# A three-column tile of norm weights padded to 32 columns in a one-core hybrid attention layer

## The chip, the core and the metric

The kernel runs on one core of one Trainium2 chip. Its time is the device time of one execution in microseconds (us); where several runs are given, their median counts.

## The reference

The reference is one layer of a generator over 1024 latent tokens with 256 context tokens in front, 1024 channels wide. The tokens are normalised and modulated, and one wide projection makes the inputs of two branches. One branch is a gated linear attention (GLA) of 4 heads, run in chunks in both directions. The other is a differential attention of 8 heads. Both are normalised, gated, projected, merged and projected once more.

```python
pl = project(modulate(x, sh_x, sc_x), w_in[layer])
pc = project(modulate(ctx, sh_c, sc_c), w_in[layer])
...
o_gla = bidir_gla(q, k, v, la_f, la_b, s_f, s_b)
o_diff = diff_attention(q1, q2, jnp.concatenate([ck1, k1], axis=2), jnp.concatenate([ck2, k2], axis=2),
                        jnp.concatenate([cv, dv], axis=2), lam)
...
a = merge_heads(rms_norm(o_gla) * gla_gain) * jax.nn.silu(gla_gate)
b = merge_heads(rms_norm(o_diff) * diff_gain * (1 - lam_init)) * jax.nn.silu(diff_gate)
y = jax.nn.sigmoid(m_gla) * (a @ w_br_gla) + jax.nn.sigmoid(m_diff) * (b @ w_br_diff)
x = x + g_x * (y @ w_out)
```

The tile that the change touches holds `gla_gain` (256 values, two columns of 128) and `diff_gain` (128 values, one column).

## The kernel before, in words

Every product of two matrices is made in float32r from operands that are split into a high and a low part: `mm3` issues three matmuls, high by high, high by low and low by high. Each matmul has a stationary operand of 128 columns, loaded into the array ahead of it (PEld in the profile), and a moving operand of mostly 512 columns, in some places 256. In the profile's names the moving operand comes first: `mm<-w,g` has the moving operand `w` and the stationary operand `g`. Numbers are left out of tile names, so `g` is a buffer of the tag `g5`, `l` of `l5`, `h` of `h0` or `h1`, `s` of `s5`, `b` of `b1`, `at` of `at4` or `at2`.

The work goes through four stages, which overlap at their edges:

- Projections (to about 500 us). `pairs` and `jobs` multiply the normalised tokens (`h0`, `h1`, `hk`) by split weights (`w`). Four of the output groups are made by a seven-product scheme on halves of the matrices, and there the stationary operands are sums of token blocks in `g5`.
- GLA and the remaining projections (about 500 to 905 us). GLA's tiles are `gv`, `gkt`, `gqe` and others; between its steps the projections `mm<-w,h` and `mm<-h,w` run.
- Differential attention (about 905 to 1450 us). Scores are `s<-hk,aq`, transposes `b<-ident,e`, products with the values `b<-at,vv`. In between run the branch projections of GLA's output, `mb<-h,wt`.
- Output (about 1450 us to the end): `mc`, `mz` and `mb` with operands `h`, `wt`, `xa`, `aq`, `ya`, `yb`, `yc`.

A driver in the kernel simulates the engines with fixed costs while the program is built, and the order of instructions on each engine comes from it. It does not look at addresses.

On-chip memory is given out by pools, which is what matters here. The pool of constants (`self.c`, pool `cst`) lies at the low end of each partition, and the pools marked `left` in `POOLS` are stacked behind it, upward: `sb` (`raw`, `h0`, `h1`), `sbK` (`hk`), `sbA` (`w`, `p`, `pl`), later `sbB` (`vv`, `at4`, `at2`, `ac`, `b1k`) and `sbC` (`ya`, `yb`, `o`). The pools marked `right` are stacked downward from the top of memory: `sbE` with one unused tile of 96 bytes, then `sbA1` (`g5`, `l5`, `x2`, `x4`), `sbA2` (GLA's tiles), `sbG` (`aq`, `xa`), `sbW` (`wt`, `ft`), `sbF` (`e5`), `sbD` (`yc`, `yd`, `wr`). Tiles start at multiples of 32 bytes.

The tile of the change, `gcol`, is filled in `consts_late` by two small DMAs, scaled there by GpSimd, and read later as a column of scales: by `pl<-tp,gcol` after GLA and by `b1k<-b,gcol` after attention.

Of the kernel before, what the change touches and what calls it, by code (L numbers as in the profile page):

```python
# [20 lines left out]
P = 128  # L21
# [211 lines left out]
class Hybrid:  # L233
# [222 lines left out]
    def consts_late(self):  # L456

        nc, a = self.nc, self.a

        def bc(ap, n):  # L460
            return ap.unsqueeze(0).to_broadcast([P, n])

        self.gains = g = self.c("gains", [P, 2, 2, 64])
        for i, nm in enumerate(("diff_q_norm", "diff_k_norm")):
            self.dma(g[:, i, 0], bc(a[nm][0], 64))
        self.gcol = self.c("gcol", [P, 3])
        self.dma(self.gcol[:, 0:2], a["gla_norm"][0].rearrange("(x p) -> p x", p=P))
        self.dma(self.gcol[:, 2:3], a["diff_norm"][0].rearrange("(x p) -> p x", p=P))
        yield from self.acq("p", 2)
        lp = self.t("p", [P, 4, 64])  # L470
        self.dma(lp, a["diff_lambda"][0].unsqueeze(0).to_broadcast([P, 4, 64]))
        yield self.d.when(lp)

        self.pool.tensor_scalar(g[:, 0, 0], g[:, 0, 0], 0.125, 0.0, ALU.mult, ALU.add)
        for i in range(2):
            gi, gr = (g[:, i, x].rearrange("p (x h e) -> p x h e", h=2, e=16) for x in range(2))
            for hh in range(2):
                self.pool.tensor_scalar(gr[:, :, hh], gi[:, :, 1 - hh], 1.0, 0.0, ALU.mult, ALU.add)
        self.pool.tensor_scalar(self.gcol[:, 0:2], self.gcol[:, 0:2], 0.5, 0.0, ALU.mult, ALU.add)
        self.pool.tensor_scalar(self.gcol[:, 2:3], self.gcol[:, 2:3], 1.0 - LAM_INIT, 0.5, ALU.mult, ALU.mult)  # L480
        lm = self.t("p", [P, 2, 64])
        self.dve.tensor_tensor(lm, lp[:, 0::2], lp[:, 1::2], ALU.mult)
        ls = self.c("ls", [P, 2])
        self.rel("p", self.dve.tensor_reduce(ls, lm, AX.X, ALU.add), 2)
        yield self.d.when(ls)
        yield self.act.activation(ls, ls, AF.Exp)
        self.nlam = self.c("nlam", [P, 1])
        self.dve.tensor_tensor(self.nlam, ls[:, 1:2], ls[:, 0:1], ALU.subtract)
        self.dve.tensor_scalar(self.nlam, self.nlam, LAM_INIT, None, ALU.subtract)
# [2321 lines left out]
```

## Time and profile before

| what | value |
|---|---|
| median of 3 runs | 1627.58 us (1626.64 to 1632.06) |
| the profiled execution's own time | 1629.48 us |
| its span in the profile | 1627.8 us |
| TensorE matmul (PE) busy | 1599.2 us, 98% |
| TensorE weight load (PEld) busy | 1328.7 us, 82% |
| VectorE (DVE) busy | 1248.3 us, 77% |
| ScalarE (ACT) busy | 858.4 us, 53% |
| GpSimd (POOL) busy | 581.7 us, 36% |
| 16 DMA engines, share of the span | 65.8% |
| granted TensorE clock | 0.997 of full |

The profile is of one execution. A row of the timeline gives the start of a batch of like instructions, its length up to the end of the last one, and their number. Since a matmul's end is modelled and it overlaps the next one, the rate of a batch is read from the start of the batch to the start of the batch behind it, divided by the number.

### The profile page before, as it was taken

To read this page: it belongs to the slowest core of one execution; us is meant where nothing else is said; L and a number is where in the kernel's file an instruction comes from. 1 tells how busy PE (TensorE), PEld (TensorE's weight loads), DVE (VectorE), ACT (ScalarE), POOL (GpSimd) and SP (SyncE) were. 2 spreads that over 40 slices of the span, in tenths; PEclk is the share of its full clock that TensorE was granted. 3 is DMA by queue.
4 is the path that set the end of the run, shared out by engine and by line. 5 is a ranking of instruction groups with operands and counts; after the bars stand their busy time and mean duration, and the time that the engine had idled before them with its cause. 6 is when DMAs were issued, how large, how long until landed. Compare 5 with 4: busy or idle time off the path is not lost.

```text
span 1627.8 us, 24787 instructions
## 1 busy us (share of the span) xinstructions
PE 1599.2 (98%) x8333; PEld 1328.7 (82%) x8333; DVE 1248.3 (77%) x2209; ACT 858.4 (53%) x1771; POOL 581.7 (36%) x631
## 2 busy tenths in 40 slices
PE   7999999999999999999999999999999999999999
PEld 3788888888888888888878788888888888887887
DVE  4687957674756889879887588787878888878994
ACT  4676644433443453565645466565665565656331
POOL 1500001000001657445554146566755666660000
PEclk9999999999999999999999999999999999999999
DMA  8576898988978577776648644454577554357662
GB/s 304 193 244 232 324 321 303 323 323 293 315 263 272 157 216 240 220 236 204 207 140 221 192 117 135 124 160 129 151 241 239 157 144 131 107 177 249 217 205 94
DMA packets 275182, 346.72 MB, mean 213 GB/s; under 512 B 24136, under 2 KB 174320, under 8 KB 275056
## 3 DMA queue, kind: packets, MB, share of 16 engines
q1 hardware_dynamic: 275056, 345.14, 65.8%
q8 instruction: 66, 1.08, 0.3%
q14 instruction: 60, 0.49, 0.1%
HBM read 235.49 MB, written 109.58 MB: 212 GB/s over the span
## 4 chain that ended last, share of the span: by engine, by line
PE 85%; DVE 5%; ACT 3%; POOL 2%; issue 2%; DMA 2%; SPq 0%; ACTq 0%; POOLq 0%; DVEq 0%
PE mm L349 30%; PE mb L349 9%; PE tp L349 7%; PE s L349 7%; PE mc L349 7%; PE b L349 6%; PE gs L349 4%; PE go L349 4%; PE b L375 4%; PE gt L349 3%; DVE sm L201 2%; PE mz L349 2%; PE tp L375 2%; ACT e L201 1%; POOL at L201 1%
## 5 line engine op out<-in xcount | busy, mean ns | idle before, releaser
L349 PE MATMUL mm<-w,h 128*128 128x512 f32 x912 | 227.6, 398 | 0.0
L349 PE MATMUL mb<-h,wt 128*128 128x512 f32 x840 | 224.2, 402 | 0.8 <-DVE ft L201 0.5
L201 ACT ACTIVATE e<-s,sm 128x1280 f32<-128x1280 f32 x128 | 169.5, 1329 | 73.7 <-DVE sm L201 70.6
L201 DVE TENSOR_REDUCE sm<-s 128x1 f32<-128x1024 f32 (+1 forms) x192 | 193.5, 1036 | 17.9 <-PE s L349 14.1
L349 PEld LDWEIGHTS mm<-w,h 128*128 128x128 f32 x912 | 167.4, 189 | 32.2
L201 POOL TENSOR_TENSOR at<-ac,at 128x512 fp32r<-128x512 f32 x128 | 188.8, 1475 | 10.7
L349 PEld LDWEIGHTS mb<-h,wt 128*128 128x128 f32 x840 | 151.2, 188 | 31.8 <-ACT ft L201 1.0
L349 PE MATMUL s<-hk,aq 128*128 128x512 f32 x744 | 170.5, 365 | 0.7 <-ACT e L201 0.4
L201 POOL TENSOR_SCALAR at<-ac 128x512 fp32r<-128x512 f32 x128 | 96.8, 756 | 194.7 <-ACT ac L201 194.5
L349 PE MATMUL mm<-h,w 128*128 128x512 f32 x672 | 165.4, 398 | 0.3 <-DVE h L201 0.3
L349 PEld LDWEIGHTS mm<-h,w 128*128 128x128 f32 x672 | 125.2, 191 | 26.5 <-DVE h L201 1.0
L349 PEld LDWEIGHTS s<-hk,aq 128*128 128x128 f32 x744 | 117.2, 188 | 18.7 <-ACT e L201 3.9
L201 DVE TENSOR_TENSOR w<-raw,w 128x512 fp32r<-128x512 f32 x128 | 89.3, 720 | 54.6 <-ACT w L201 54.2
L349 PE MATMUL b<-at,vv 128*128 128x256 f32 x960 | 130.1, 287 | 1.1 <-ACT ac L201 0.8
L201 POOL TENSOR_TENSOR sm<-sm,nhalf 128x2 f32<-128x2 f32 (+2 forms) x94 | 108.0, 1149 | 44.7 <-DVE sm L201 39.5
L349 PEld LDWEIGHTS b<-at,vv 128*128 128x128 f32 x960 | 119.8, 191 | 3.0 <-ACT ac L201 1.0
L201 DVE SCALAR_TENSOR_TENSOR e<-e,sm,e 128x1280 f32<-128x1280 f32 x64 | 120.3, 1879 | 0.7
L201 ACT ACTIVATE ac<-b 128x512 f32<-128x512 f32 x122 | 72.1, 597 | 81.9 <-PE b L375 81.5
L201 ACT ACTIVATE w<-raw 128x512 fp32r<-128x512 f32 x128 | 76.8, 625 | 65.7 <-DMA raw<-in_w_in 18.7
L349 PE MATMUL mm<-w,g 128*128 128x512 f32 x432 | 108.9, 396 | 0.0
L349 PEld LDWEIGHTS mm<-w,g 128*128 128x128 f32 x432 | 81.0, 187 | 20.2 <-issue 0.5
L201 ACT ACTIVATE p<-mm 128x512 f32<-128x512 f32 (+1 forms) x104 | 60.2, 586 | 69.1 <-PE mm L349 54.3
(352 smaller groups left out, 3102.8 us busy)
## 6 DMA issues: line engine op xcount, KB each, us to landing
raw<-in_w_in SPq DMA_DIRECT2D x62, 512.0 KB, 5.2
g<-d_s SPq DMA_DIRECT2D x32, 640.0 KB, 6.8
gv<-d_v SPq DMA_DIRECT2D x80, 256.0 KB, 3.9
g<-d_s SPq DMA_DIRECT2D x32, 512.0 KB, 6.2
aq<-d_qT SPq DMA_DIRECT2D x124, 128.0 KB, 3.4
d_dv<-pl SPq DMA_DIRECT2D x40, 256.0 KB, 4.1
d_v<-pl SPq DMA_DIRECT2D x40, 256.0 KB, 2.6
d_kT<-pl SPq DMA_DIRECT2D x40, 256.0 KB, 2.7
```

The source lines that it names most:

```text
L201: self.ins = f(out, *args, **kw).ins
L349: self.ins = self.nc.tensor.matmul(out, lhsT, rhs, start=start, stop=stop, skip_group_check=more).ins
L375: self.nc.tensor.transpose(out, src, self.ident[:n, :n])
```

## The change

The tile `gcol` is made 32 columns wide instead of three: 128 bytes per partition instead of 12. The three columns in use, the two DMAs into them and every instruction that reads them stay.

```diff
-        self.gcol = self.c("gcol", [P, 3])
+        self.gcol = self.c("gcol", [P, 32])
         self.dma(self.gcol[:, 0:2], a["gla_norm"][0].rearrange("(x p) -> p x", p=P))
         self.dma(self.gcol[:, 2:3], a["diff_norm"][0].rearrange("(x p) -> p x", p=P))
```

The order of instructions is the same on all five engines (PE 6622 rows, DVE 2064, ACT 1405, POOL 607, SP 1077). What moves is memory. The 12 bytes took 32, the 128 bytes take 128, so that everything behind `gcol` in the constants (`ls`, `nlam`) and every tile of every left pool lies 96 bytes higher. The tiles of the right pools, the constants ahead of `gcol` (`ident`, `ones`, `cs`, `gains` and others) and the accumulators stay where they were. These are the byte offsets in a partition as the built program has them:

```
                      before     mod 64  mod 256     after      mod 64  mod 256
gcol                  3648       0       64          3648       0       64
raw (first)           5280       32      160         5376       0       0
h0 (first)            17568      32      160         17664      0       0
h1 (first)            50336      32      160         50432      0       0
hk                    83104      32      160         83200      0       0
w (first)             109728     32      160         109824     0       0
pl (first)            146592     32      160         146688     0       0
g5 (first)            162176     0       128         162176     0       128
aq (first)            192384     0       128         192384     0       128
wt (first)            208768     0       128         208768     0       128
```

All large buffers are a multiple of 512 bytes long, so all buffers of a tag, and the column blocks that the matmuls take from them, share the remainders of the first. The 8155 matrix instructions of the program have 2560 float32r matmuls with 512 moving columns and 128 stationary ones that take one operand from a left pool and one from a right pool (2416 with the moving one on the left, 144 with it on the right), 2552 that take both from left pools and 16 that take both from right pools.

## The prediction

> **What bounds the kernel now.** I read the page's engine table and chain first, then the busy time by stage, then the timeline of PE, batch by batch.
>
> ```profile
> PE 1599.2 (98%) x8333; PEld 1328.7 (82%) x8333; DVE 1248.3 (77%) x2209; ACT 858.4 (53%) x1771; POOL 581.7 (36%) x631
> PE 85%; DVE 5%; ACT 3%; POOL 2%; issue 2%; DMA 2%; SPq 0%; ACTq 0%; POOLq 0%; DVEq 0%
> ```
>
> The first line is busy time by engine, the second the chain that ended last. PE is busy for 98% of the span, so only a change of PE's own rate can move the time by much. By stage (time, then PE, PEld, DVE, ACT, POOL busy with instruction counts, clock, DMA share, GB/s):
>
> ```profile
> 100.00:200.00 100.00, 100.00 (x441) 81.86 (x440) 82.90 (x129) 65.30 (x95) 0.99 (x1) 1.00 0.79 281
> 300.00:400.00 100.00, 100.00 (x434) 81.21 (x434) 61.96 (x98) 39.76 (x68) 0.00 (x0) 1.00 0.87 314
> 500.00:905.00 405.00, 400.24 (x2138) 340.30 (x2137) 325.19 (x631) 207.55 (x552) 205.84 (x264) 1.00 0.71 213
> 905.00:1450.00 545.00, 538.83 (x3259) 464.08 (x3258) 447.94 (x816) 329.14 (x667) 330.79 (x295) 1.00 0.52 151
> 1450.00:1628.00 178.00, 171.87 (x774) 140.29 (x773) 138.01 (x233) 68.43 (x134) 10.28 (x10) 1.00 0.59 202
> ```
>
> The projections have no PE gap at all; attention leaves 545.00 - 538.83 = 6.2 us, the output stage 6.1 us. The clock is full, so a matmul's pace isn't throttled.
>
> The next view is the one on which everything rests: the timeline of PE in the output stage, where batches of like matmuls run without a gap. All have 512 moving columns; the first name is the moving operand, the second the stationary one.
>
> ```profile
> 1535.54 11.36 PE L349 MATMUL mc<-wt,h 128*128 128x512 f32 x48
> 1546.74 11.07 PE L349 MATMUL mc<-h,ya 128*128 128x512 f32 x48
> ...
> 1590.61 5.60 PE L349 MATMUL mz<-h,yb 128*128 128x512 f32 x24
> 1596.05 2.88 PE L349 MATMUL mc<-h,yb 128*128 128x512 f32 x12
> 1598.77 2.89 PE L349 MATMUL mb<-h,yb 128*128 128x512 f32 x12
> 1601.50 5.76 PE L349 MATMUL mz<-h,yc 128*128 128x512 f32 x24
> 1607.10 2.96 PE L349 MATMUL mc<-h,yc 128*128 128x512 f32 x12
> ```
>
> From start to start, `mz<-h,yb` takes (1596.05 - 1590.61)/24 = 226.7 ns each, and `mz<-h,yc` (1607.10 - 1601.50)/24 = 233.3 ns, with the same accumulator tag, the same kind of moving operand and nothing waited for. `h` and `yb` are both left tiles, 32 mod 64; `yc` is a right tile, 0 mod 64. It is not the side of the moving operand: `mc<-wt,h`, moving from the right and stationary from the left, also takes (1546.74 - 1535.54)/48 = 233.3. In the projections the same two rates stand side by side:
>
> ```profile
> 276.24 2.88 PE L349 MATMUL tp<-w,h 128*128 128x512 f32 x12
> 278.96 2.88 PE L349 MATMUL gs<-w,h 128*128 128x512 f32 x12
> ...
> 287.22 2.26 PE L349 MATMUL mm<-w,g 128*128 128x512 f32 x9
> 289.32 0.86 PE L349 MATMUL gs<-w,g 128*128 128x512 f32 x3
> ```
>
> `tp<-w,h` (left, left) takes 2.72/12 = 226.7, `mm<-w,g` (left, right) 2.10/9 = 233.3. So a matmul whose operands differ by 32 bytes mod 64 takes 6.67 ns longer than one whose operands agree. That is my reading, and its weak point is that in this kernel "differ by 32" and "one from each end of memory" are the same matmuls.
>
> **The change, part by part.** After it every left tile is 0 mod 64, as every right tile already is, so all 2560 left-right matmuls agree. The rows that hold them (the first five of the whole program, the last two of 905 to 1450 us):
>
> ```profile
> L349 PE MATMUL mm<-w,g 128*128 128x512 f32 x432 | 108.9, 396 | 0.0
> L349 PE MATMUL gs<-w,g 128*128 128x512 f32 x144 | 41.4, 395 | 0.0
> L349 PE MATMUL tp<-w,g 128*128 128x512 f32 x120 | 29.5, 394 | 0.0
> L349 PE MATMUL gt<-w,g 128*128 128x512 f32 x96 | 23.7, 395 | 0.0
> L349 PE MATMUL go<-w,g 128*128 128x512 f32 x72 | 20.7, 395 | 0.0
> ...
> L349 PE MATMUL mb<-h,wt 128*128 128x512 f32 x816 | 218.3, 402 | 0.8 <-DVE ft L201 0.5 <-ACT ft L201 0.2
> L349 PE MATMUL s<-hk,aq 128*128 128x512 f32 x496 | 139.1, 401 | 0.5 <-ACT e L201 0.4
> ```
>
> *Projections*: 432 + 144 + 120 + 96 + 72 = 864 matmuls, 864 x 6.67 = 5.8 us. PE never waits there, nothing can swallow it, and I take all of it.
>
> *Attention*: 816 + 496 and 6 of `mc<-h,wt` at the end of this stretch = 1318, worth 8.8 us. Here PE trades work with ACT, DVE and POOL all the time, and DVE's 447.94 us of 545 leaves it no bound of its own but many hand-overs: PE gains, arrives earlier, and waits for a split or a softmax that comes when it came. Of each hand-over it keeps something between all and nothing. With gaps of only 6.2 us now I take two thirds, 5.9 us; the bounds are 0 and 8.8.
>
> *Output*: the other 2560 - 864 - 1318 = 378, worth 2.5 us. PE is busy 171.87 of 178, and I take nine tenths, 2.3 us; bounds 0 and 2.5.
>
> *GLA* has no left-right matmul, but its short batches alternate between left pairs and right pairs (five rows of the timeline, then three groups of 500 to 905 us):
>
> ```profile
> 743.56 0.71 PE L349 MATMUL go<-gv,gso 128*128 128x256 f32 x3
> 744.11 0.86 PE L349 MATMUL mm<-w,h 128*128 128x512 f32 x3
> 744.81 1.60 PE L349 MATMUL tp<-gv,gkt 128*128 128x256 f32 x12
> 746.25 4.94 PE L349 MATMUL mm<-w,h 128*128 128x512 f32 x21
> 751.02 1.17 PE L349 MATMUL gs<-gqr,gkk 128*128 128x64 f32 x9
> ...
> L349 PE MATMUL mm<-w,h 128*128 128x512 f32 x768 | 193.0, 399 | 0.0
> L349 PE MATMUL mm<-h,w 128*128 128x512 f32 x288 | 71.5, 395 | 0.0
> L349 PE MATMUL mm<-w,hk 128*128 128x512 f32 x96 | 24.3, 397 | 0.0
> ```
>
> The batch of three at 744.11, between two right pairs, runs at 0.70/3 = 233.3, the batch of 21 at 4.77/21 = 227.1. So changing over between remainders costs too, and after the change there is nothing to change over. Of the 768 + 288 + 96 = 1152 matmuls I guess that a third stand in such short batches: 384 x 6.67 = 2.6 us. GLA has waits of its own, so I take half, 1.3 us; bounds 0 and 2.6.
>
> *Matmuls of 256 columns*: `tp<-gv,gkt`, two right tiles, takes (746.25 - 744.81)/12 = 120.0 ns. The row of two left tiles is
>
> ```profile
> 86.34 4.48 PE L349 MATMUL mm<-hk,w 128*128 128x256 f32 x36
> 90.66 0.39 PE L349 MATMUL gs<-l,l 128*128 128x512 f32 x1
> 90.89 0.40 PE L349 MATMUL go<-l,l 128*128 128x512 f32 x1
> ```
>
> with 4.32/36 = 120.0 as well. Two operands at 0 run like two at 32, which is what the left pairs need in order to keep their rate. I cost them at nothing.
>
> *The other engines and the DMAs* read and write the moved tiles too:
>
> ```profile
> L201 ACT ACTIVATE w<-raw 128x512 fp32r<-128x512 f32 x128 | 76.8, 625 | 65.7 <-DMA raw<-in_w_in 18.7 <-PE go L349 15.9 <-PE gs L349 12.5
> L201 ACT ACTIVATE w<-l 128x512 fp32r<-128x512 f32 x30 | 17.9, 624 | 14.5 <-PE gs L349 7.8 <-PE go L349 6.7
> l<-in_w_ada SPq DMA_DIRECT2D x4, 512.0 KB, 7.5
> raw<-in_w_ada SPq DMA_DIRECT2D x4, 512.0 KB, 6.1
> ```
>
> ACT reads `raw` (32 mod 64) in 625 ns and `l` (0 mod 64) in 624: no difference. Loads of the same source land in 6.1 us at 32 and 7.5 us at 0; they were issued at other moments, so they prove no gain, and if the remainder did cause the 23%, it would lie beside a PE that is busy 100.00 us of 100. I take zero for both. The wider `gcol` itself is read one column at a time as before: zero.
>
> *Sum*: 5.8 + 5.9 + 2.3 + 1.3 = 15.3 us. The profiled execution's own time, 1629.48 us (span 1627.8), becomes 1614.2; the median, 1627.58, lies 1.9 below it, and with the same difference taken off becomes 1612.3 us.
>
> **The rivals.**
>
> *Nothing changes.* The 6.67 ns may belong to the two ends of memory and not to the remainder, or operands may have to agree mod 256, where left would be 0 and right 128 after the change. Then every left-right matmul stays at 233.3 and the time at 1627.6. For it: no row shows a left-right matmul whose operands agree. Against it: the border would have to lie between the highest left weights (`pl`, ending at 154784) and the lowest `g5` (162176), just where the kernel happens to divide its memory, while `h0` at 17568 and `w` at 146592 go together at full rate. I give it 0.12. A page of the Trainium skill leads to this rival by another way. TensorE: Matmul & The Clock Gate, section Part 2: What happens when you issue a matmul, says that PE reads moving data and weights through two independent ports, so that loading weights takes no bandwidth from the running matmul. By that rule the weights' address could not matter and the sum would be 0; the rows at 226.7 and 233.3, with nothing but the stationary tile changed, disagree.
>
> *Slower.* Agreement may be the wrong word: perhaps a matmul is quick only with both operands at 32, and 512 columns at 0 and 0 run at 233.3. Then the 2552 left pairs lose 2552 x 6.67 = 17.0 us, the mixed ones gain nothing, and the time is 1644.6; it decides as soon as a left pair loses more than a mixed one wins, since the two kinds are about equally many. For it: the only right pairs of 512 columns, `gs<-l,l` above, take 230 ns (90.89 - 90.66), not 226.7. Against it: these stand alone between left pairs, where the change-over is paid, and the right pairs of 256 columns settle at the left pairs' 120.0. I give it 0.05.
>
> *The gain is handed to the waits.* Attention, GLA and output give all of it back, and the projections alone keep theirs: 1627.6 - 5.8 = 1621.8. It is the upper end of my own case, since it is still faster.
>
> **How the numbers follow.** About 0.3% (4.9 us) is what a measurement of this kernel can tell from no change. My case, 1612.3, has 0.83; its whole span, from 1627.58 - 5.8 - 8.8 - 2.5 - 2.6 = 1607.9 to 1621.8, lies below 1622.7 and so counts as faster. The first rival is "same", the second "slower". The range is that span; the two rivals, 0.17, are left out.
>
> **What would show it.** In the timeline after, `mz<-h,yc` and `mc<-wt,h` at 226.7 ns per matmul and `mm<-w,g` at 2.04 us for 9, with `mz<-h,yb` still at 226.7. PE's busy time some 15 us less; the gaps of PE in 905 to 1450 us larger by about 3 us than 6.2. If mixed batches still run at 233.3, the remainder mod 64 isn't the cause; if `mz<-h,yb` goes up, agreement isn't; if all run at 226.7 and the time has not fallen, the hand-overs were mis-sized.

## The result and the profile after

The padded kernel takes 1627.0 us (median of 12 runs, 1624.8 to 1631.18) beside 1629.55 us for the kernel before (12 runs, 1626.63 to 1632.06): a ratio of 0.9989, 95% interval 0.9978 to 1.0. That lies within 0.3% of no change. The forecast of 1612.3 us and its whole range, 1607.9 to 1621.8, are missed. Of the prediction's cases, the first rival, "nothing changes", came true.

These are the engine table and the chain's shares of the kernel after:

```profile
PE 1598.2 (98%) x8333; PEld 1329.6 (82%) x8333; DVE 1249.4 (77%) x2209; ACT 857.8 (53%) x1771; POOL 583.2 (36%) x631
PE 85%; DVE 6%; ACT 3%; POOL 3%; issue 2%; DMA 1%; SPq 0%; ACTq 0%; POOLq 0%; DVEq 0%
```

PE's busy time fell by 1.0 us, where some 15 were forecast. By stage, the second numbers are PE's busy time and instructions:

```profile
300.00:400.00 100.00, 100.00 (x435) 81.58 (x435) 61.67 (x97) 39.89 (x68) 0.00 (x0) 1.00 0.85 309
905.00:1450.00 545.00, 538.36 (x3260) 464.47 (x3259) 448.79 (x820) 330.05 (x671) 333.82 (x297) 1.00 0.51 151
```

In 300 to 400 us PE has no gap and starts 435 matmuls, one more than before. In attention its gaps are 545.00 - 538.36 = 6.6 us, against 6.2 before. So the time isn't lost to new waits: there was hardly any gain to lose. The timeline of PE in the output stage, after, says why:

```profile
1533.66 11.35 PE L349 MATMUL mc<-wt,h 128*128 128x512 f32 x48
1544.85 11.06 PE L349 MATMUL mc<-h,ya 128*128 128x512 f32 x48
...
1588.67 5.60 PE L349 MATMUL mz<-h,yb 128*128 128x512 f32 x24
1594.11 2.88 PE L349 MATMUL mc<-h,yb 128*128 128x512 f32 x12
...
1599.56 5.75 PE L349 MATMUL mz<-h,yc 128*128 128x512 f32 x24
1605.14 2.95 PE L349 MATMUL mc<-h,yc 128*128 128x512 f32 x12
```

From start to start, `mz<-h,yb` (left, left) still takes 5.44/24 = 226.7 ns, `mz<-h,yc` (left, right) 5.58/24 = 232.5 and `mc<-wt,h` 11.19/48 = 233.1. All these operands are now 0 mod 64, and the mixed pairs are as slow as they were. This is the case that the prediction named in its last part: the remainder mod 64 isn't the cause. Two explanations stay: the two ends of memory, or agreement over a larger modulus (before 160 and 128 mod 256, after 0 and 128).

### The profile page after: what moved, and what is told of

Read it like the earlier page. It is cut to its first block, busy times and chain, and to the rows that moved or that the text cites. A ratio compares the mean times of both kernels' runs of the same rounds, so it can differ in the third digit from the quotient of the medians.

```text
span 1625.8 us, 24787 instructions
## 1 busy us (share of the span) xinstructions
PE 1598.2 (98%) x8333; PEld 1329.6 (82%) x8333; DVE 1249.4 (77%) x2209; ACT 857.8 (53%) x1771; POOL 583.2 (36%) x631
## 4 chain that ended last, share of the span: by engine, by line
PE 85%; DVE 6%; ACT 3%; POOL 3%; issue 2%; DMA 1%; SPq 0%; ACTq 0%; POOLq 0%; DVEq 0%
PE mm L349 29%; PE mb L349 9%; PE s L349 7%; PE tp L349 7%; PE mc L349 7%; PE b L349 6%; PE gs L349 4%; PE b L375 4%; PE go L349 4%; PE gt L349 3%; DVE sm L201 2%; PE mz L349 2%; PE tp L375 2%; ACT e L201 1%; POOL at L201 1%
```

## The experiments

In three kernels a series of matmuls of the same shape as the kernel's runs alone. Each matmul has its stationary operand at one byte offset of a partition and its moving operand at another. Nanoseconds per matmul are from the start of a batch to the start of the next, divided by its count.

### Which addresses are slow

The moving operand lies at A, the stationary one at B, 48 matmuls a batch:

```python
for a, b in CONF:                      # pairs of byte offsets
    for r in range(16):
        sh, sl, mh, ml = at(b, 128), at(b + 2048, 128), at(a, 512), at(a + 2048, 512)
        nc.tensor.matmul(pt, sh, mh, ...); nc.tensor.matmul(pt, sh, ml, ...); nc.tensor.matmul(pt, sl, mh, ...)
```

> Not the layer: matmuls alone (512 columns, 128 weights, float32r, three per step with two moving and two stationary blocks), 48 in a batch, 30 batches back to back, each with other addresses of the moving (A) and the stationary operand (B); the output is left out. Theory 1, agreement modulo a power of two above 64: A = 16384 with B = 32768 + d runs at 226.7 ns for d = 0 and at about 233 ns for d below that power; far apart but with d = 0 (B = 65536 to 196608) it runs at 226.7 everywhere. Theory 2, the two ends of memory: B = 32768 + d runs at 226.7 for every d, and with growing distance there is an address from which B (A staying at 16384) runs at 233; both operands above it run at 226.7 again. The six pairs of addresses taken from the kernels must give the 226.7 and 233.3 that their traces show, or the batches are no stand-in.

| A, B | ns per matmul |
|---|---|
| 16384, 32768 (the run's first batch; its last 36 gaps, since the first ones take up to 591 ns) | 226.7 |
| 16384, 32768 + 16 | 226.9 |
| 16384, 32768 + 32 and + 64 | 233.1, 233.3 |
| 16384, 32768 + 128 | 232.5 |
| 16384, 32768 + 256, 512, 1024, 4096, 8192 | 226.7 to 226.8 |
| 16384, B from 65536 to 196608 (8 batches, all 0 mod 256) | 226.7 each |
| moving operand between 98304 and 196608, stationary one at 16384, 163840 or 196608 (6 batches, all 0 mod 256) | 226.7 to 226.9 |
| 17568, 109728 (`h`, `w` before, both 160 mod 256) | 227.7 |
| 109728, 162176 (`w`, `g` before) and 109824, 162176 (after) | 233.3, 233.3 |
| 17568, 208768 (`h`, `wt` before) and 17664, 208768 (after) | 233.3, 233.3 |
| 208768, 17568 (`wt`, `h` before; the run's last batch, 47 gaps) | 233.4 |

The two ends of memory are refuted: 16384 and 196608 go together at full pace. What counts is the remainder of the distance, and 256 bytes is the modulus, since 64 and 128 are slow and 256 is quick. A page of the Trainium skill that the prediction weighed, TensorE: Matmul & The Clock Gate (section Part 2: What happens when you issue a matmul), gives the running matmul and the weight load two independent read ports. By that rule B could not matter; here moving B by 64 bytes and nothing else costs 6.6 ns. Another page, SBUF — State Buffer (section Operand start alignment), says of its rule on operand starts that it is about legality and that its runs timed nothing; here the address, legal everywhere, does have a price.

### The kernel with agreement, made in two ways

Both start from the kernel before and change the unused tile at the top of memory, which moves the right tiles alone. With 64 bytes they lie 32 higher and both sides have 160 mod 256, but differ mod 512. With 832 bytes `aq`, `wt` and `yc` lie so that they agree with the left tiles up to mod 2048.

```diff
-    EDGE = 96
+    EDGE = 64      # e1
+    EDGE = 832     # e2
```

> The kernel before with the unused right-hand tile at 64 instead of 96 bytes: right tiles move up by 32, so left and right tiles agree modulo 256 (160 and 160), not modulo 512. Theory 1 with a power up to 256: left-right matmuls at 226.7 ns and 12 to 18 us less, ratio 0.989 to 0.993. Theory 1 with a higher power, or theory 2: they stay at 233 ns, ratio 0.997 to 1.003.

> The kernel before with the unused right-hand tile at 832 bytes: right tiles move down by 736, so that wt, aq and yc agree with the left tiles modulo 2048 (1184), and g5 modulo 512. Theory 1 with any power up to 512: left-right matmuls at 226.7 ns, ratio 0.989 to 0.993; with 1024 or 2048, mb<-h,wt and mc<-h,yc fall to 226.7 and mm<-w,g does not in every buffer. Theory 2: all left-right matmuls at 233 ns, ratio 0.997 to 1.003.

The first took 1618.4 us (ratio 0.9935, 0.992 to 0.995), the second 1619.19 (0.9943, 0.9927 to 0.996), beside 1628.05 before. The timeline of the first in the output stage:

```profile
1525.40 11.04 PE L349 MATMUL mc<-wt,h 128*128 128x512 f32 x48
1536.29 11.04 PE L349 MATMUL mc<-h,ya 128*128 128x512 f32 x48
...
1590.68 5.60 PE L349 MATMUL mz<-h,yc 128*128 128x512 f32 x24
1596.12 2.88 PE L349 MATMUL mc<-h,yc 128*128 128x512 f32 x12
```

Now `mc<-wt,h` takes 10.89/48 = 226.9 and `mz<-h,yc` 5.44/24 = 226.7. Agreement mod 256 is enough; agreeing further gains nothing that these runs can tell. That operands which agree make the kernel faster, as I predicted, is so, and it is worth about 0.6%: 9.7 and 8.9 us, where I had expected 12 to 18 of the first and a ratio of 0.989 to 0.993 of both.

### The rule, distance by distance

The same series with more distances d of B from a multiple of 256, with both operands at the same remainder r, with 256 and 128 moving columns, with batches that change over between remainders 0 and 128 every k matmuls, and with transposes in between.

> Not the layer: batches of 48 matmuls as in the first run of this kind, the output left out. Theory (operand starts must agree modulo 256 bytes, to within one 16-byte line): d, the distance modulo 256 of the stationary from the moving operand, at 0, 4, 8, 16, 240 and 256 gives 226.7 ns, at 48, 64, 96, 128, 160, 192, 224 gives 233.3; 4 and 8 bytes stay inside a line, 20 bytes may go either way. Equal remainders other than 0 (32, 128, 160 for both operands) give 226.7; if the remainder itself mattered, they would not. With 256 columns agreeing operands take 120.0 ns, disagreeing ones 117 to 120. Change-over: alternating single matmuls, threes, sixes and twelves between agreeing pairs at remainder 0 and 128 takes more than 226.7 each, most for the short ones (230 to 234 for threes, 228 or less for twelves); with all at one remainder 226.7. Four transposes and four 512-column matmuls in turn: the batch is shorter when identity, transposed tile and matmul operands all have one remainder than with the identity at 0 and the rest at 160, by 5 to 40 ns per turn; rival: transposes do not care, and the batches are equal.

The timeline of this kernel; the name says the distance (d), the common remainder (r), the moving columns (q: 256), and how often it changes over (al, alt):

```profile
80.97 11.36 PE L81 MATMUL dthirtytwo<-mem 128*128 128x512 f32 x48
92.16 11.36 PE L81 MATMUL dfortyeight<-mem 128*128 128x512 f32 x48
...
181.22 11.05 PE L81 MATMUL dtwofiftysix<-mem 128*128 128x512 f32 x48
192.11 11.07 PE L81 MATMUL rthirtytwo<-mem 128*128 128x512 f32 x48
203.02 11.10 PE L81 MATMUL ronetwentyeight<-mem 128*128 128x512 f32 x48
...
224.86 5.91 PE L81 MATMUL qzero<-mem 128*128 128x256 f32 x48
230.62 5.83 PE L81 MATMUL qthirtytwo<-mem 128*128 128x256 f32 x48
236.29 5.86 PE L81 MATMUL qonetwentyeight<-mem 128*128 128x256 f32 x48
241.99 5.47 PE L81 MATMUL ozero<-mem 128*128 128x128 f32 x48
...
269.41 11.41 PE L81 MATMUL althree<-mem 128*128 128x512 f32 x48
280.66 11.15 PE L81 MATMUL altsix<-mem 128*128 128x512 f32 x48
291.65 11.08 PE L81 MATMUL altwelve<-mem 128*128 128x512 f32 x48
```

A distance of 32 takes 11.19/48 = 233.1 ns, 256 takes 226.9, both operands at 32, 128 and 160 take 227.3, 227.9 and 227.1. In the same way the distances 48, 64, 160 and 224 give 233.1 to 233.4, 96 gives 234.2, 128 gives 232.5, 192 gives 229.2, 4, 8, 16 and 20 give 232.5, 230.6, 233.3 and 232.9, and 240 gives 226.7. My expectation that distances within 16 bytes run at full pace is missed at 4, 8 and 16, and that 192 is as slow as the others is missed too. With 256 columns there is no such price: 120.0, 118.1 and 118.8 ns at distances 0, 32 and 128. Changing over every three matmuls between pairs that agree at 0 and at 128 takes 11.25/48 = 234.4, so a change-over costs (234.4 - 226.7) x 3 = 23 ns there; every six it takes 10.99/48 = 229.0, which makes 14 ns each, so the price isn't one number. Turns of four transposes and four matmuls took 171.0 to 171.3 ns an instruction wherever the identity lay.

### Three more ways to agree in the kernel

All operands and the transposes' identity at 0 mod 256; all at 32; and the change of this case made twice as wide, so that left and right tiles are both at 128 while `ident` stays at 0.

```diff
 # e3, from the kernel after
-    EDGE = 96
+    EDGE = 224
 # e4, from the kernel after
-    EDGE = 96
+    EDGE = 192
+        self.c("shift", [P, 8])          # ahead of ident
 # e5, from the kernel before
-        self.gcol = self.c("gcol", [P, 3])
+        self.gcol = self.c("gcol", [P, 64])
```

> The changed kernel with the unused right-hand tile at 224 instead of 96 bytes: left tiles, right tiles and the identity all at 0 modulo 256. Theory: left-right matmuls of 512 columns at 226.7 ns, and no change-over any more, neither between left and right pairs nor between transposes and matmuls: ratio 0.986 to 0.992, 2 to 10 us below the kernel with the 64-byte tile (1618.4). Rival, the change-over costs nothing: the same time as with the 64-byte tile, ratio 0.992 to 0.995.

> The changed kernel with a 32-byte tile put ahead of the identity and the right-hand tile at 192 bytes: left tiles, right tiles and the identity all at 32 modulo 256. Theory, only agreement counts: the time of the kernel with all at 0, to within 0.2%. Rival, starts at multiples of 256 (or of 64) help the DMAs or the engines by themselves: slower than that by 0.3% or more.

> The edit of the change taken further: gcol with 64 columns (256 bytes), everything else as before: left tiles at 128 modulo 256 like the right tiles, the identity at 0. Theory: 226.7 ns for the left-right matmuls, ratio 0.991 to 0.995 as with the 64-byte tile; the change-over to the identity stays, so slower than the kernel with all at 0. Rival, agreement needs 512: ratio 0.997 to 1.003.

Beside 1628.23 us before they took 1617.27 (0.9929, 0.9917 to 0.9941), 1619.23 (0.9941, 0.9929 to 0.9954) and 1619.3 (0.9946, 0.9934 to 0.9958). All five versions that agree are faster than both kernels, and their intervals overlap: neither the common remainder nor the identity's place is shown to matter. I had expected the version at 0 to lie 2 to 10 us below 1618.4, because it has no change-over left; it lies 1.1 below, so the rival of that expectation, a change-over that costs the kernel nothing, stands. The engine table and the output stage of the first of them:

```profile
PE 1587.3 (98%) x8333; PEld 1328.0 (82%) x8333; DVE 1249.1 (77%) x2209; ACT 858.0 (53%) x1771; POOL 582.2 (36%) x631
```

```profile
1526.05 11.04 PE L349 MATMUL mc<-wt,h 128*128 128x512 f32 x48
1536.93 11.04 PE L349 MATMUL mc<-h,ya 128*128 128x512 f32 x48
...
1591.33 5.60 PE L349 MATMUL mz<-h,yc 128*128 128x512 f32 x24
1596.77 2.88 PE L349 MATMUL mc<-h,yc 128*128 128x512 f32 x12
```

PE is busy 11.9 us less than before (1599.2 to 1587.3), and both operands at 0 run at 10.88/48 = 226.7 ns. That also settles the rival that ended slower: 512 columns at 0 and 0 are as quick as at 160 and 160.

### Why attention gains so little

With true agreement the attention stage gained 1.0 to 1.6 us (the table of stretches below), less than a fifth of the 8.8 us that 1318 matmuls at 6.67 ns make. The last kernel puts n matmuls of 512 columns behind four transposes, or behind matmuls of 256 columns, six turns each, with operands that agree or lie 128 ("half") or 224 ("off") apart. It also runs the distance 16 once behind a quick batch and once behind a slow one, since the first two series gave 226.9 and 233.3 for it.

> Not the layer: matmul batches as before, the output left out. Question 1, why attention kept so little: turns of four transposes and n matmuls of 512 columns (n = 4, 12, 18), and turns of four or twelve 256-column matmuls and three or six of 512, with operands that agree modulo 256 (agree), are 128 off (half) or 224 off (off). Theory A: after a transpose or another width the pace has to settle, so short batches pay whatever the addresses are: n = 4 agree and off differ by under 10 ns per turn, n = 18 by 60 ns or more. Theory B: every disagreeing matmul pays its 6.67 ns: 27 ns per turn at n = 4, 80 at 12, 120 at 18. With the 512-column operands agreeing among themselves at another remainder (other) than the 256-column ones, theory of the change-over between remainders: longer than agree by 10 to 25 ns per turn; theory A: under 5. Question 2, the line of 16 bytes: 8, 16, 240 and 192 bytes off, each once behind a batch that agrees and once behind one that is 64 off. If the pace is a state that a batch takes over from the one ahead, 16 and 240 give 226.7 behind an agreeing batch and 233 behind the other; if the address alone decides, both give the same.

Its timeline. A name with "tm" is a turn with transposes, and the number is n; for "qm" the turns have 4 matmuls of 256 columns and 3 of 512, or 12 and 6. The six turns of such a name stand in one row, under the form of the first matmul. "other" are 512-column operands that agree with each other, at 160, between 256-column ones that agree at 0.

```profile
36.45 11.04 PE L89 MATMUL dsixteen<-mem 128*128 128x512 f32 x48
47.33 11.37 PE L89 MATMUL dsixtyfour<-mem 128*128 128x512 f32 x48
58.53 11.37 PE L89 MATMUL dsixteenb<-mem 128*128 128x512 f32 x48
69.74 11.06 PE L89 MATMUL dzerob<-mem 128*128 128x512 f32 x48
...
213.24 0.60 PE L87 MATMUL tmfouragree<-identa,mem 128*128 128x128 f32 x4
...
221.46 0.60 PE L87 MATMUL tmtwelveagree<-identa,mem 128*128 128x128 f32 x4
...
240.68 0.60 PE L87 MATMUL tmeighteenagree<-identa,mem 128*128 128x128 f32 x4
...
268.06 7.15 PE L89 MATMUL qmthreeagree<-mem 128*128 128x256 f32 x42
275.04 17.09 PE L89 MATMUL qmsixagree<-mem 128*128 128x256 f32 x108
291.97 0.60 PE L87 MATMUL tmfourhalf<-identa,mem 128*128 128x128 f32 x4
...
300.17 0.60 PE L87 MATMUL tmtwelvehalf<-identa,mem 128*128 128x128 f32 x4
...
319.57 0.60 PE L87 MATMUL tmeighteenhalf<-identa,mem 128*128 128x128 f32 x4
...
347.37 7.18 PE L89 MATMUL qmthreehalf<-mem 128*128 128x256 f32 x42
354.38 17.08 PE L89 MATMUL qmsixhalf<-mem 128*128 128x256 f32 x108
371.30 0.60 PE L87 MATMUL tmfouroff<-identa,mem 128*128 128x128 f32 x4
...
450.60 7.16 PE L89 MATMUL qmthreeother<-mem 128*128 128x256 f32 x42
457.60 17.04 PE L89 MATMUL qmsixother<-mem 128*128 128x256 f32 x108
474.47 1.56 PE L89 MATMUL last<-mem 128*128 128x512 f32 x6
```

A turn is a sixth of the way to the next name. With 4 matmuls it takes 8.22/6 = 1.37 us where they agree and 8.20/6 = 1.37 where they don't; with 12 it takes 3.20 and 3.23; with 18, 4.56 and 4.63. The single starts of the trace show how: behind transposes the first gap between matmuls is 314 to 322 ns in every case. Where operands agree, the next gaps vary between 224 and 236 ns, 232 on average, and only then they stay at 226 to 227; turn by turn it is five or six such gaps, then nine, then five or six again. Where operands don't agree, the gaps vary around 233 to the end. Three and six matmuls behind 256 columns gain nothing (6.98 and 7.01 us, 16.93 and 16.92), and a change-over to another common remainder costs nothing there (7.00 and 16.87). So in the series agreement pays from the seventh, eighth or eleventh matmul of 512 columns in a row. In the kernel the first four `mb<-h,wt` of a row gain nothing (231.9 ns before, 232.7 with all operands at 0), the fifth to the tenth go from 233.4 to 229.4, and the later ones from 233.2 to 227.4.

## Why the prediction was wrong, point by point

**The step that failed is the reading "differ by 32 bytes mod 64".** The rows of before fitted every power of two from 64 to 512 alike, because left and right were 160 and 128 mod 256, and 160 and 384 mod 512; I took the smallest, and the change agrees by that one alone. The modulus is 256 (128 apart 232.5 ns, 256 apart 226.7), so the operands went from a distance of 224 to one of 128, from one slow distance to another. I had named this case, in one rival with the two ends of memory, and argued only against the ends. The first half of that rival is refuted and the second shown.

**The terms**, measured where the operands truly agree. PE's stretches between the same instructions of the program, from the starts in the traces, in us:

| stretch | before | after | the five that agree | gain | predicted |
|---|---|---|---|---|---|
| first `mm<-w,g` to last `gs<-w,g` | 322.0 | 321.9 | 316.4 to 317.1 | 4.9 to 5.6 | 5.8 |
| to the first `s<-hk,aq` | 404.7 | 405.2 | 402.8 to 406.4 | -1.7 to 1.9 | 1.3 |
| to the last `b<-at,vv` | 548.3 | 548.0 | 546.7 to 547.3 | 1.0 to 1.6 | 5.9 |
| to the end | 160.6 | 161.1 | 158.6 to 158.7 | 1.9 to 2.0 | 2.3 |

- *Projections and output* were sized about rightly for operands that truly agree (the change itself brought neither): 864 matmuls in long rows, and an output stage with hardly a gap. All 432 of `mm<-w,g` go from a mean of 233.3 to 226.7 ns.
- *Attention* was mis-sized, and for another reason than the one that I discounted for. Its gaps did grow, from 6.2 us to 7.7, as the row of this stage in the version with all operands at 0 shows, but that is 1.5 us, where the forecast was about 3:

```profile
905.00:1450.00 545.00, 537.30 (x3270) 464.91 (x3270) 449.76 (x826) 329.61 (x673) 338.62 (x303) 1.00 0.51 152
```

  The 6.67 ns themselves are not there in short rows: of 840 `mb<-h,wt` only 124 stand behind the tenth matmul of an unbroken row of 512 columns, and of 496 `s<-hk,aq` 15. Those 124 go from 233.2 to 227.4 ns; the earlier ones from 232.8 to 230.7, and the earlier `s<-hk,aq` from 232.6 to 231.7. Taken from the starts of every matmul in the two traces, leaving out gaps of 260 ns and more, that makes some 2.7 us, not 8.8, and the longer waits take a part of it back.
- *GLA's change-over*, which the prediction put at 1.3 us, isn't seen. `mm<-w,h` within the first ten of a row takes 230.4 ns before, over the whole program, and 230.4 in the version at 0. A change-over between remainders does cost, 14 and 23 ns in the series above, but there both sides have 512 columns. In GLA the neighbours have 256, 128 or 64 columns, and behind 256 columns the last series shows short batches as slow without a change-over as with one. The batch of three that the prediction read as the sign of a change-over, at 744.11 before, stands at 738.80 in the version at 0, where there is none, and still takes 0.70/3 = 233.3 ns; that reading was wrong:

```profile
738.80 0.86 PE L349 MATMUL mm<-w,h 128*128 128x512 f32 x3
739.50 1.59 PE L349 MATMUL tp<-gv,gkt 128*128 128x256 f32 x12
```

- *256 columns, the identity, the other engines and the DMAs*, costed at nothing: the series show no price for the first two, and ACT's busy time of 857.8 us after and 858.0 in the version at 0 stands beside 858.4.

**The remaining 0.1%** of the kernel after isn't explained. Its pace did change a little with the new distance: all `mm<-w,g` fell from 233.3 to 232.5 ns and `mb<-h,wt` from 232.9 to 232.4, and the series give 232.5 for 128 apart and 233.1 for 224. Over the 2560 mixed matmuls it is 0.5 ns on average, about 1.2 us, which fits PE's busy time. But the series at the kernel's own addresses showed 233.3 for both, and the stretches of the table don't show a gain: together they are 0.6 us longer after than before. In the traces the whole difference lies ahead of the first `mm<-w,g`, which starts at 189.6 us after and 192.2 before, and at 188.8 to 192.1 in the five. The interval reaches 1.0, so an effect of this distance on the time isn't shown.

**What stays open** is what in the chip makes 256 bytes the period, why a row needs six to ten matmuls to settle, and why this number alternates from turn to turn.

## What to carry to other kernels

Where TensorE is the bound and long rows of 512-column float32r matmuls run, look at the start of the moving and of the stationary operand modulo 256 bytes: a tile of some hundred bytes in the constants moves everything behind it, and here 128 bytes more in the unused tile at the top, added to this change, gave 0.9929 of the time before, 11 us, where this change alone gave nothing that can be told. When two groups of rows differ in pace and their addresses differ, list every modulus that fits the rows before choosing one; a change that satisfies the smallest alone is a bet. And a price per instruction that was read in long uniform rows need not hold in short mixed ones; here attention kept less than a fifth of it.

## What the runs showed of the hardware

- A 512-column float32r matmul takes 226.7 ns where both operands start at the same remainder mod 256 bytes, and 232.5 to 234.2 ns at distances from 32 to 160 and at 224; with 256 columns the distance shows no price.
- Near agreement there is memory in it: 16 bytes apart takes (47.33 - 36.45)/48 = 226.7 ns behind a quick batch and (69.74 - 58.53)/48 = 233.5 behind a slow one, and goes on so for all 48. At 240 it was 226.7 and 228.3, though in the series before it 226.7 also behind a slow batch (224 apart). At 8 and 192 the batch ahead made no difference: 230.8 and 230.6, 229.0 and 229.2.
- Behind four transposes, six, seven or ten matmuls of operands that agree pass before the quick pace is reached, with gaps of 224 to 236 ns after the first.
